# Attention blocks spread over the next projection, with longer rests before their products, in a decoder trunk on one core

## The chip, the cores and the metric

The kernel runs on one core of one Trainium2 chip. The metric is the device time of one execution in microseconds (us), from a median of runs. TensorE (PE in the rows, its weight loads PEld), VectorE (DVE), ScalarE (ACT) and GpSimd (POOL) each work through their own list of instructions; SyncE (SP) issues the DMA transfers.

## The reference, cut to what matters

One decoder layer on 2048 rows of width 1024. The normalised input is projected to 4096 columns, which feed two kinds of head: four HGRN2 heads of 128 (group A) and eight stick-breaking attention heads of 64 (group B). Both outputs are normalised per head, gated, and go through one output projection; a gated embedding is added and a last normalisation ends the layer.

```
# group B: stick-breaking attention, strictly causal
z        = q k^T / 8
log_1m   = where(mask, -softplus(z), 0)
log_rest = cumsum(log_1m, reverse) - log_1m
w        = where(mask, exp(log_sigmoid(z) + log_rest), 0)
o        = w v
# group A: HGRN2, state of 128 x 128 per head
S_t = diag(f_t) S_{t-1} + k_t v_t^T ;  o_t = S_t^T q_t ;  k_t = 1 - f_t
```

## The kernel before, in words

The rows are turned round, so that each query looks forward, and cut into four chunks of 512 (`c` = 3, 2, 1, 0). The 4096 projected columns are cut into eight groups `g` of 512, by turns a pair of B heads and one A head. A **unit** is one group on one chunk: there are 32, four of B, four of A, four of B and so on. Every matmul of f32 numbers is made of three matmuls of f16 parts (high by high, high by low, low by high).

A unit's own work is its **projection** (`proj_A`, `proj_B`): 48 matmuls of 512 columns in `proj_t` and 96 of 256 columns in `proj_n`, written into the PSUM tiles `pj`. What follows on it, the **mix** (`mix_A`, `mix_B`), is written as a Python generator and is emitted piece by piece between the matmuls of the *next* unit's projection. A small planner does this while the program is written. `clock` counts the time of the matmuls emitted so far (columns / 2400 + 0.003 us each, in `mm`). A `yield 4.0` of a generator puts its next piece at least 4.0 of that clock later. `step_tasks` emits the first task whose time has come, and `run` calls it after each step of the projection. A `Task` bears the number of the unit it may run in, and after each projection `drain(u)` emits everything that is still left of that unit's tasks, moving `clock` forward where the next piece isn't due.

The emission order is not the last word: the Tile layer under it orders each engine's instructions once more, by emission and by when it expects their inputs.

`mix_B` works in four blocks of 128 queries. `block(b)` computes two heads' scores `z` against a window of 320 keys (4 matmuls or 8), four sigmoids on ACT (L619, L620), a scan (L624) and a product (L629) on DVE, a cast on ACT (L632), two subtractions on POOL (L634, L636), and a DMA that transposes the weights `wt` into `at` (L638). Then it rests 12.5, and the block's **product** with the values goes into the PSUM tile `op`. Blocks are emitted 4.0 apart. After the fourth product, `finish()` normalises: a square on ACT that reads `op` (L657), a sum on DVE (L659), a power on POOL (L84), a multiplication on POOL (L662) and one on DVE that reads `op` for the last time (L664, into `y_t`). `op` has one buffer (`ps_o`, `bufs=1`), shared by all units of both kinds; `wt` and `at` have two each.

`mix_A` goes through seven levels (12 matmuls `lps` each), with a rest of 2.2 after each, then a transposing DMA of `kp` into `at`, a rest of 6.5, the state matmuls `sp`, and four steps into `op`.

Tasks that prepare weights (`weight_piece`, `prepare_task`) and the input (`prep_x`, in the first four units) run in the same way. After the 32 units a final stage (matmuls `np`) computes the output projection, the embedding and the last normalisation.

Of the kernel before, what the change touches and what calls it, by code (L numbers as in the profile page):

```python
# [8 lines left out]
F32 = mybir.dt.float32  # L9
# [8 lines left out]
P = 128  # L18
# [15 lines left out]
def trunk_kernel(  # L34
# [134 lines left out]
        clock[0] += 0.109  # L169

    class Task:
        def __init__(self, gen, after):
            self.gen, self.ready, self.unit = gen, clock[0] + after, unit[0]

    tasks = []
    unit = [0]

    def spawn(gen, after=0.0):
        tasks.append(Task(gen, after))

    def step_tasks(last):

# [300 lines left out]
    def mix_A(h, c, kq, f_, vh, vl, gs):  # L483
        k_, q_ = kq[:, 0, :], kq[:, 1, :]
        kqf = kq.rearrange("p i t -> p (i t)")
        sc = f32("sc", (P, CB, P))
        pr_ = sc.rearrange("p b t -> p (b t)")
        kp2_ = [f16(f"kp{i}", (P, 2, CH)) for i in range(2)]
        kp = [(t[:, 0, :], t[:, 1, :]) for t in kp2_]
        nc.gpsimd.memset(kp2_[0], 0.0)  # L490
        nc.gpsimd.tensor_tensor(pr_, q_, k_, op=ALU.mult)
        split(kp[1][0], kp[1][1], k_, p2(SKB))
        nc.vector.tensor_tensor(q_, q_, f_, op=ALU.mult)
        v4 = lambda t, B: t.rearrange("p (n h b) -> p n h b", h=2, b=B)
        q3 = lambda t, B: t.rearrange("p (n b) -> p n b", b=B)
        T = {0: f_}
        qc = {}

        def parts(lv):
            B = 1 << lv  # L500
            qc[lv] = f16("qch", (P, CH // 2)), f16("qcl", (P, CH // 2))
            split(q3(qc[lv][0], B), q3(qc[lv][1], B), v4(q_, B)[:, :, 0, :], p2(SQF))
            if lv > 0:
                kh, kl = kp[(lv + 1) % 2]
                split(v4(kh, B)[:, :, 1, :], v4(kl, B)[:, :, 1, :], v4(k_, B)[:, :, 1, :], p2(SKB))

        def update(lv):

            B = 1 << lv
            nb = CH // (2 * B)  # L510
            T2 = T[lv].rearrange("p (n h) -> p n h", h=2)
            act = kqf[:, B : 2 * CH - B].rearrange("p (i m b) -> p i m b", i=2, b=B)[:, :, ::2, :]
            other = T[lv].rearrange("p (n h) -> p h n", h=2).unsqueeze(3).broadcast_to([P, 2, nb, B])
            nc.vector.tensor_tensor(act, act, other, op=ALU.mult)  # L514
            T[lv + 1] = wk.tile([P, nb], F32, name="Tn", tag=f"T{lv}")
            nc.vector.tensor_tensor(T[lv + 1], T2[:, :, 0], T2[:, :, 1], op=ALU.mult)  # L516

        parts(0)
        update(0)
        prh, prl = f16("qh"), f16("ql")  # L520
        split(prh, prl, pr_, p2((SQF + 4)))
        nc.gpsimd.memset(sc, 0.0)
        yield 2.0
        for lv in range(NLEV):
            B = 1 << lv
            kh, kl = kp[(lv + 1) % 2]
            qch, qcl = qc.pop(lv)
            lps = pa("lps", (P, CB, 64))
            for b in range(CB):
                r_ = slice(b * P, (b + 1) * P)  # L530
                s2 = slice(b * 64, (b + 1) * 64)
                mm3(lps[:, b, :], [(kh[:, r_], qch[:, s2]), (kh[:, r_], qcl[:, s2]), (kl[:, r_], qch[:, s2])])
            if lv == 4:
                dps = pa("dps", (P, CB, P))
                mm3(dps, [(ones16, prh), (ones16, prl)])
                nc.vector.copy_predicated(sc, ident.bitcast(I32).unsqueeze(1).broadcast_to([P, CB, P]), dps)
            dst = sc.rearrange("p c (n h b) -> p c n h b", h=2, b=B)[:, :, :, 0, :]
            msk = masks[:, lv, :].bitcast(I16)
            if lv == 0:
                nc.vector.copy_predicated(dst[:, :, :, 0], msk.unsqueeze(1).broadcast_to([P, CB, 64]), lps)  # L540
            elif B == 64:
                nc.vector.copy_predicated(dst[:, :, 0, :], msk.unsqueeze(1).broadcast_to([P, CB, 64]), lps)
            else:
                m4 = q3(msk, B).unsqueeze(1).broadcast_to([P, CB, 64 // B, B])
                nc.vector.copy_predicated(dst, m4, lps.rearrange("p c (n b) -> p c n b", b=B))  # L545
            if lv + 1 < NLEV:
                parts(lv + 1)
                update(lv + 1)
            yield 2.2
        qh, ql = f16("qh"), f16("ql")  # L550
        split(qh, ql, q_, p2(SQF))
        scs = f16("wt", (P, 2, CB, P))
        sch, scl = scs[:, 0], scs[:, 1]
        split(sch, scl, sc, p2(SS - SQF - SKB))
        split(kp[0][0], kp[0][1], k_, p2(SKB))
        ktt = f16("at", (P, 2, CB, P))
        nc.sync.dma_start(ktt.rearrange("p l b d -> p (l b) d"), kp2_[0].rearrange("p l t -> p (l t)"), transpose=True)
        kth, ktl = ktt[:, 0], ktt[:, 1]
        yield 6.5
        sp = ps_t.tile([P, CB, P], F32, name="sp", tag="t")  # L560
        for b in reversed(range(CB)):
            mm3(sp[:, b, :], [(kth[:, b, :], vh[:, b, :]), (kth[:, b, :], vl[:, b, :]), (ktl[:, b, :], vh[:, b, :])])
        op = ps_o.tile([P, CB, P], F32, name="op", tag="o")
        first = c == NC - 1
        if first:
            state[h] = wk.tile([P, P], F32, name="st_")
        st_ = state[h]
        ss = small("ssA", CB)
        for b in reversed(range(CB)):
            r_ = slice(b * P, (b + 1) * P)  # L570
            start_ = first and b == CB - 1
            pairs = [(sch[:, b, :], vh[:, b, :]), (sch[:, b, :], vl[:, b, :]), (scl[:, b, :], vh[:, b, :])]
            if start_:
                nc.vector.tensor_copy(st_, sp[:, b, :])
            else:
                sh = wk.tile([P, P], F16, name="sh", bufs=2)
                sl = wk.tile([P, P], F16, name="sl", bufs=2)
                split(sh, sl, st_, p2(SS - SQF - SKB))
                pairs += [(qh[:, r_], sh), (qh[:, r_], sl), (ql[:, r_], sh)]
                nc.vector.scalar_tensor_tensor(st_, st_, T[NLEV][:, b : b + 1], sp[:, b, :], op0=ALU.mult, op1=ALU.add)  # L580
                yield 1.2
            mm3(op[:, b, :], pairs)
            junk = f16("jk", (P, P))
            nc.scalar.activation(junk, op[:, b, :], AF.Square, accum_out=ss[:, b : b + 1])
        r = rsqrt(ss, CB, 1.0 / P, EPS * p2(2 * (SS + SV)))
        y = f32("y", (P, CB, P))
        for b in range(CB):
            nc.vector.scalar_tensor_tensor(y[:, b, :], op[:, b, :], r[:, b : b + 1], gs[:, b, :], op0=ALU.mult, op1=ALU.mult)
        yield 5.0
        y_out(y, h, c)  # L590
        done(h, c)
# [2 lines left out]
    ZS = p2(-SQ - SK) / 8.0  # L594

    def mix_B(pr, c, qs, kt, gs):
        op = ps_o.tile([P, CB, 2, 64], F32, name="op", tag="o")
        left = [CB]

        def block(b):  # L600
# [35 lines left out]
                nc.gpsimd.tensor_tensor(wt[:, :, WB : 3 * P], sg[:, :, 2 * P :], wt[:, :, 2 * P : WB], op=ALU.subtract)  # L636
            at = f16("at", (P, 2, 5, P))
            nc.sync.dma_start(at.rearrange("p h j t -> p (h j) t"), wt.rearrange("p h s -> p (h s)"), transpose=True)  # L638
            yield 12.5
            for hd in range(2):  # L640
                cols = slice(64 * hd, 64 * hd + 64)
                ah = at[:, hd]
# [9 lines left out]
                spawn(finish())  # L652

        def finish():
            sqt = f32("sc", (P, CB * 2, 64))
            op8 = op.rearrange("p b h d -> p (b h) d")
            nc.scalar.activation(sqt, op8, AF.Square)  # L657
            ss = small("ssB", CB * 2)
            nc.vector.tensor_reduce(ss, sqt, axis=AX, op=ALU.add)  # L659
            r = rsqrt(ss, CB * 2, 1.0 / 64, EPS * p2(2 * (SA + SV)))  # L660
            gr = gs.rearrange("p b (h d) -> p (b h) d", h=2)
            nc.gpsimd.tensor_tensor(gr, gr, r.unsqueeze(2).broadcast_to([P, CB * 2, 64]), op=ALU.mult)  # L662
            y = f32("y", (P, CB, P))
            nc.vector.tensor_tensor(y.rearrange("p b (h d) -> p (b h) d", h=2), op8, gr, op=ALU.mult)  # L664
            yield 7.0
            y_out(y, 4 + pr, c)
            done(4 + pr, c)

        for b in reversed(range(CB)):
            spawn(block(b))  # L670
            yield 4.0


    fin = {}
# [150 lines left out]
    for u, (g, c) in enumerate(order):  # L825
# [2 lines left out]
            w_new(g + 1)  # L828
        for n in ([c - 1, c - 2] if u == 0 else [c - 2]):
            if g == 0 and n >= 0:  # L830
                spawn(prep_x(n), 0.0 if n == c - 1 else 12.0)
        spawn(weight_piece(g + 1, range(KD * i0 // NC, KD * (i0 + 1) // NC)), 3.0)
        kind, i = groups[g]
        unit[0] = u + 1
        run((proj_A if kind == "A" else proj_B)(u, g, i, c), u)
        drain(u)
        if g == 7 and i0 < 3 and c > 0:
            w_new(9 + i0)
            spawn(prepare_task(9 + i0), 0.5)

    for n in range(9, 12):
        if n not in ws:
# [160 lines left out]
```

## Time and profile before

| | us |
|---|---|
| median of 3 runs (lowest, highest) | 1299.4 (1298.64, 1300.02) |
| the profiled execution | 1299.25 |
| its span, first to last instruction | 1297.5 |
| PE busy in the span | 1223.2 |
| DVE, ACT, POOL busy | 870.6, 593.2, 372.5 |

Busy time of PE has modelled ends, since matmuls are pipelined: a 512-column matmul is shown 0.38 us long, while the next starts 0.216 us after it. The stages, by the tiles on PE: start until 50 us, the first B group (with the input's preparation) to 185, A to 280, B to 400, A to 497, B to 610, A to 710, B to 822, the last A group to 960, the final stage to 1290.

### The profile page before, as it was taken

The numbers are of one execution on the slowest core, as the hardware profiler recorded it, in microseconds if no ns is written. First come the engines' busy times: TensorE is split into PE (matmuls) and PEld (weight loads), VectorE is DVE, ScalarE is ACT, GpSimd is POOL, SyncE is SP. The second block draws the span as 40 slices with busy tenths as digits, with TensorE's granted clock in tenths as the row PEclk, the third lists the DMA queues.
The fourth block names the chain that finished last, engine by engine and source line by source line (L and its number), as shares of the span: only waits on it lengthen the run. The fifth ranks groups of instructions, "written<-read, shape, count | busy, mean of one in ns | idle before, by whom it ended". The sixth has DMA issues, their size and how long they took to land.

```text
span 1297.5 us, 25819 instructions
## 1 busy us (share of the span) xinstructions
PE 1223.2 (94%) x9802; PEld 774.3 (60%) x9802; DVE 870.6 (67%) x1736; ACT 593.2 (46%) x1507; POOL 372.5 (29%) x472
## 2 busy tenths in 40 slices
PE   8887989999999999999999999898999999999997
PEld 7655657666666767665776666565544444444443
DVE  5769779986578997567999566799854424324233
ACT  7655534554353454454455444456443323223222
POOL 4247531114442113445111354301022211211112
PEclk9999999999999999999999999999999999999998
DMA  9877640256571025656005557634628226213111
GB/s 262 275 183 182 170 91 14 47 140 134 108 195 28 18 82 131 138 131 139 18 18 135 131 123 171 165 93 141 153 49 186 86 62 154 73 49 110 46 49 52
DMA packets 268964, 147.03 MB, mean 113 GB/s; under 512 B 213280, under 2 KB 237856, under 8 KB 268832
## 3 DMA queue, kind: packets, MB, share of 16 engines
q1 hardware_dynamic: 268688, 145.04, 45.4%
q8 instruction: 79, 1.29, 0.4%
q14 instruction: 53, 0.43, 0.1%
q10 hardware_dynamic: 144, 0.26, 0.1%
HBM read 52.44 MB, written 33.55 MB: 66 GB/s over the span
## 4 chain that ended last, share of the span: by engine, by line
PE 35%; DVE 30%; DMA 13%; issue 7%; ACT 7%; SPq 4%; POOL 3%; ACTq 0%; DVEq 0%; POOLq 0%
PE np L160 27%; PE pj L160 7%; DMA at_t<-wt_t 4%; DVE kq_t L514 4%; DVE kp_t L77 3%; DVE e_t L624 3%; DMA at_t<-kp_t 3%; DVE wl L133 2%; DVE sc_t L545 2%; DVE qcl_t L77 2%; DVE e_t L629 2%; DMA raw_t<-w_in 1%; DVE Tn L516 1%; DVE ys_t L77 1%; POOL wt_t L634 1%
## 5 line engine op out<-in xcount | busy, mean ns | idle before, releaser
L160 PE MATMUL pj<-wh,xh 128*128 128x256 f16 x1024 | 282.6, 276 | 3.1 <-DVE ql_t L77 3.1
L160 PE MATMUL pj<-wh,xl 128*128 128x256 f16 x1024 | 282.4, 276 | 0.0
L160 PE MATMUL pj<-wl,xh 128*128 128x256 f16 x1024 | 282.4, 276 | 0.0
L160 PEld LDWEIGHTS <-xh 128*128 128x128 f16 x2048 | 200.1, 99 | 28.6 <-issue 0.3
L160 PE MATMUL pj<-xh,wh 128*128 128x512 f16 (+1 forms) x560 | 198.3, 365 | 7.5 <-DVE gs_t L389 2.2
L160 PE MATMUL pj<-xl,wh 128*128 128x512 f16 (+1 forms) x560 | 199.0, 365 | 4.2 <-DVE xl L260 3.4
L160 PE MATMUL pj<-xh,wl 128*128 128x512 f16 (+1 forms) x560 | 198.9, 365 | 0.0
L160 PEld LDWEIGHTS <-wh 128*128 128x128 f16 x1120 | 104.4, 99 | 96.3 <-issue 11.9
L160 PEld LDWEIGHTS <-at_t 128*128 128x128 f16 x1688 | 97.3, 98 | 106.6 <-DMA at_t<-wt_t 33.2
L84 POOL TENSOR_TENSOR rs_y<-rs_v,mhalf 128x1 f32<-128x1 f32 (+2 forms) x87 | 82.5, 948 | 269.2 <-DVE rs_v L83 267.1
L160 PE MATMUL np<-wh,fy 128*128 128x512 f16 x512 | 155.7, 379 | 0.0
L160 PEld LDWEIGHTS <-fy 128*128 128x128 f16 x768 | 74.4, 98 | 87.9
L764 DVE TENSOR_TENSOR e_t<-e_t,kq_t 128x512 f32<-128x512 f32 (+2 forms) x33 | 22.3, 675 | 137.4 <-POOL kq_t L763 137.3
L160 PEld LDWEIGHTS <-xl 128*128 128x128 f16 x1024 | 101.3, 99 | 19.9 <-issue 3.8
L624 DVE TENSOR_TENSOR_SCAN e_t<-e_t,reset 128x642 f32<-128x642 f32 x56 | 87.7, 1567 | 24.0 <-ACT e_t L619 23.4
L160 PE MATMUL np<-wh,at_t 128*128 128x512 f16 (+2 forms) x264 | 98.0, 373 | 0.0
L160 PE MATMUL np<-wl,at_t 128*128 128x512 f16 (+2 forms) x264 | 98.0, 373 | 0.0
L160 PE MATMUL np<-wh,wt_t 128*128 128x512 f16 (+2 forms) x264 | 97.9, 373 | 0.0
L160 PE MATMUL np<-wl,fy 128*128 128x512 f16 x256 | 97.0, 379 | 0.0
L76 ACT ACTIVATE qch_t<-kq_t 128x256 f16<-128x256 f32 x112 | 46.8, 418 | 106.2 <-DVE kq_t L514 88.6
L632 ACT CAST wt_t<-e_t 128x640 f16<-128x640 f32 (+1 forms) x64 | 44.9, 701 | 99.5 <-DVE e_t L629 62.0
L634 POOL TENSOR_TENSOR wt_t<-e_t,wt_t 128x512 f16<-128x512 f32 (+1 forms) x64 | 78.1, 1220 | 39.2 <-ACT wt_t L632 39.2
(193 smaller groups left out, 2305.1 us busy)
## 6 DMA issues: line engine op xcount, KB each, us to landing
raw_t<-w_in SPq DMA_DIRECT2D x61, 256.0 KB, 3.6
raw_t<-x_nat SPq DMA_DIRECT2D x56, 256.0 KB, 3.8
out<-y_t SPq DMA_DIRECT2D x31, 256.0 KB, 2.1
kq_t<-x_t SPq DMA_DIRECT2D x12, 512.0 KB, 5.1
bkv<-kn_t SPq DMA_DIRECT2D x64, 64.0 KB, 2.0
bkv<-ql_t SPq DMA_DIRECT2D x64, 64.0 KB, 2.0
bkv<-bkv SPq DMA_DIRECT2D x64, 64.0 KB, 2.3
gs_d<-gs_t SPq DMA_DIRECT2D x16, 256.0 KB, 3.0
```

Of the source, the lines that this page charges most:

```text
L76: nc.scalar.activation(hi, src, AF.Copy, scale=scale)
L77: nc.vector.scalar_tensor_tensor(lo, src, scale, hi, op0=ALU.mult, op1=ALU.subtract)
L84: nc.gpsimd.tensor_tensor(y, v, mhalf[:, 0:n], op=ALU.pow)
L133: nc.vector.scalar_tensor_tensor(self.l[:, k, :], self.r[k], g, self.h[:, k, :], op0=ALU.mult, op1=ALU.subtract)
L160: nc.tensor.matmul(out_, lhsT, rhs, start=start, stop=stop)
L514: nc.vector.tensor_tensor(act, act, other, op=ALU.mult)
L545: nc.vector.copy_predicated(dst, m4, lps.rearrange("p c (n b) -> p c n b", b=B))
L624: nc.vector.tensor_tensor_scan(fl(pr_), fl(f), fl(reset), 0.0, op0=ALU.mult, op1=ALU.max)
L629: nc.vector.tensor_tensor(sg[:, :, :w_], sg[:, :, :w_], pr_[:, :, :w_], op=ALU.mult)
L632: nc.scalar.copy(wt[:, :, :w_], sg[:, :, :w_])
L634: nc.gpsimd.tensor_tensor(wt[:, :, 3 * P : 3 * P + lw], sg[:, :, :lw], wt[:, :, :lw], op=ALU.subtract)
L764: nc.vector.tensor_tensor(h_, h_, p_, op=ALU.add)
```

## The change

Three things are changed in the planner's program; no computation is changed.

1. Rests. `mix_B`: blocks 6.0 apart instead of 4.0, and 16.0 instead of 12.5 between a block's transposing DMA and its product. `mix_A`: 2.4 instead of 2.2 after each of seven levels, 7.0 instead of 6.5 ahead of the state matmuls.
2. The limit. `drain(u - 1)` instead of `drain(u)`: what is left of a mix when its unit ends is emitted within the following unit's projection, and is drained a unit later. Weights and input preparation get `early=1`, and so keep their old limit.
3. `op` of `mix_B` is made at the first product, not at the start of `mix_B`.

```
-        def __init__(self, gen, after):
-            self.gen, self.ready, self.unit = gen, clock[0] + after, unit[0]
+        def __init__(self, gen, after, early):
+            self.gen, self.ready, self.unit = gen, clock[0] + after, unit[0] - early
...
-    def spawn(gen, after=0.0):
-        tasks.append(Task(gen, after))
+    def spawn(gen, after=0.0, early=0):
+        tasks.append(Task(gen, after, early))
... mix_A
-            yield 2.2
+            yield 2.4
...
-        yield 6.5
+        yield 7.0
... mix_B
-        op = ps_o.tile([P, CB, 2, 64], F32, name="op", tag="o")
+        op_ = []
...
-            yield 12.5
+            yield 16.0
+            if not op_:
+                op_.append(ps_o.tile([P, CB, 2, 64], F32, name="op", tag="o"))
+            op = op_[0]
...
         for b in reversed(range(CB)):
             spawn(block(b))
-            yield 4.0
+            yield 6.0
... the loop over units
-                spawn(prep_x(n), 0.0 if n == c - 1 else 12.0)
-        spawn(weight_piece(g + 1, range(KD * i0 // NC, KD * (i0 + 1) // NC)), 3.0)
+                spawn(prep_x(n), 0.0 if n == c - 1 else 12.0, 1)
+        spawn(weight_piece(g + 1, range(KD * i0 // NC, KD * (i0 + 1) // NC)), 3.0, 1)
...
         run((proj_A if kind == "A" else proj_B)(u, g, i, c), u)
-        drain(u)
+        drain(u - 1)
         if g == 7 and i0 < 3 and c > 0:
             w_new(9 + i0)
-            spawn(prepare_task(9 + i0), 0.5)
+            spawn(prepare_task(9 + i0), 0.5, 1)
```

## Rows read from the trace of the kernel before

**Rows 1.** The page: the span, and TensorE's busy time, share, instructions.

```profile
span 1297.5 us, 25819 instructions
PE 1223.2 (94%) x9802; PEld 774.3 (60%) x9802; DVE 870.6 (67%) x1736; ACT 593.2 (46%) x1507; POOL 372.5 (29%) x472
```

**Rows 2.** Busy time by stage: B first, B, A, B, last A, final stage.

```profile
core 0: us, PE busy (x) PEld busy (x) DVE busy (x) ACT busy (x) POOL busy (x), PEclk, DMA share, GB/s
50.00:185.00 135.00, 112.90 (x934) 75.05 (x933) 100.62 (x140) 71.12 (x164) 69.19 (x81) 0.97 0.71 179
280.00:400.00 120.00, 111.85 (x959) 75.87 (x958) 77.83 (x114) 55.76 (x139) 52.75 (x73) 0.97 0.59 135
400.00:497.00 97.00, 95.79 (x997) 69.85 (x996) 91.49 (x225) 48.67 (x136) 14.28 (x13) 1.00 0.21 53
...
710.00:822.00 112.00, 104.53 (x941) 72.61 (x940) 67.94 (x103) 52.23 (x132) 49.28 (x68) 1.00 0.61 135
822.00:960.00 138.00, 130.16 (x1109) 81.31 (x1108) 122.48 (x285) 73.82 (x190) 21.12 (x19) 0.98 0.53 133
960.00:1290.00 330.00, 328.21 (x1555) 150.22 (x1552) 121.13 (x251) 101.23 (x250) 64.58 (x76) 1.00 0.34 84
```

**Rows 3.** Waits of TensorE, whole span: total us, times, longest us.

```profile
PE op L160 <- DMA at_t<-wt_t: 25.3, 21, 3.3
PE op L160 <- DVE y_t L664: 5.6, 3, 2.4
PE lps L160 <- ACT kp_t L76: 4.3, 7, 2.6
...
PE sp L160 <- DMA at_t<-kp_t: 1.9, 4, 0.6
```

**Rows 4.** Timeline near 750 us: one block's scores, its transposing DMA's issue, its product.

```profile
743.74 0.72 PE L160 MATMUL z<-bkv,qs_t 128*128 128x256 f16 x8
...
751.86 1.41 SPq L638 DMA_TRANSPOSE at_t<-wt_t  x1
...
756.26 0.63 PE L160 MATMUL op<-bkv,at_t 128*128 128x64 f16 x16
```

**Rows 5.** Timeline, the block two later: scores, DMA issue, last projections, product.

```profile
752.44 0.71 PE L160 MATMUL z<-bkv,qs_t 128*128 128x320 f16 x4
...
763.14 1.35 SPq L638 DMA_TRANSPOSE at_t<-wt_t  x1
...
765.14 0.38 PE L160 MATMUL pj<-xl,wh 128*128 128x512 f16 x1
766.61 0.26 PE L160 MATMUL op<-bkv,at_t 128*128 128x64 f16 x3 [1.09 <-DMA at_t<-wt_t]
```

**Rows 6.** Timeline from a unit's last product to the next unit's first.

```profile
741.53 0.64 PE L160 MATMUL op<-bkv,at_t 128*128 128x64 f16 x16 [0.71 <-DMA at_t<-wt_t]
...
742.53 0.59 ACT L657 ACTIVATE sc_t<-op 128x512 f32<-128x512 f32 x1
...
748.34 0.68 DVE L664 TENSOR_TENSOR y_t<-op,gs_t 128x512 f32<-128x512 f32 x1
...
751.97 0.63 PE L160 MATMUL op<-bkv,at_t 128*128 128x64 f16 x16
```

**Rows 7.** Timeline, the same pair of events where the chain is slow.

```profile
362.21 0.43 PE L160 MATMUL z<-bkv,qs_t 128*128 128x320 f16 x2
...
366.72 0.63 PE L160 MATMUL op<-bkv,at_t 128*128 128x64 f16 x16
...
381.36 0.67 DVE L664 TENSOR_TENSOR y_t<-op,gs_t 128x512 f32<-128x512 f32 x1
...
382.09 0.84 PE L160 MATMUL op<-bkv,at_t 128*128 128x64 f16 x16 [2.37 <-DVE y_t L664]
```

**Rows 8.** Busy time and granted clock just behind two waits.

```profile
337.95:341.36 3.41, 3.41 (x10) 1.21 (x9) 1.80 (x2) 1.19 (x2) 2.04 (x2) 0.50 0.15 58
382.32:385.74 3.42, 3.42 (x41) 2.75 (x38) 3.42 (x5) 1.10 (x2) 2.19 (x3) 0.50 0.24 58
```

More of the change, by code (lines that the diff above doesn't have):

```diff
@@ L654, in finish @@
         def finish():
+            op = op_[0]
             sqt = f32("sc", (P, CB * 2, 64))
```

## The prediction

> **What bounds the kernel now.** The page comes first: TensorE is busy for 94% of the span [rows 1], so the question is where the other 74 us lie, and whether the change touches them. The view by stage answers the first part [rows 2]. In the final stage PE is busy for 328 of 330 us, and in the A group from 400 to 497 us for 95.8 of 97: there is next to nothing to win there. In the B groups it is busy for 111.9 of 120 and 104.5 of 112 us, and in the first one for 112.9 of 135. So a B group loses some 7 to 8 us of idle PE, the first one 22, and the last A group 8. The same rows show who could take PE's place: in the A group DVE is busy for 91.5 of 97 us, in the B groups for 61 to 65% only.
>
> The view of waits names what ends PE's idle time [rows 3]. The largest entry by far is the product of an attention block that waits for its transposed weights: 25.3 us in 21 waits, the longest 3.3. The product that waits for `y_t`, that is for the single `op` buffer to be read out by the unit before, comes next with 5.6 us in 3 waits.
>
> The timeline shows why. One block's scores start at 743.74 and its product at 756.26 [rows 4]: 12.52 us, which is the planner's rest of 12.5. So the place of a product on PE is set by the rest, as long as PE runs at the planner's pace. Two blocks later the scores start at 752.44, but the transposing DMA is issued only at 763.14, 10.7 us later, and the product waits for it until 766.61, that is 14.2 us after its scores [rows 5]. The rest is thus about as long as the work that it is to cover, and any delay on DVE, ACT, POOL or SP on the way lands on PE. Everything behind the product on PE (the next projection) waits too.
>
> **The change part by part.** The times are summed against the profiled execution's own 1299.25 us, which stands 0.15 us under the median of 1299.4.
>
> *Longer rest and wider spacing in mix_B.* With 16.0 the product stands some 3.5 us later in PE's order, behind projection matmuls that are ready. The longest wait of the 21 is 3.3 us [rows 3], so if the weights arrive no later than now, every one of them is covered. Blocks 6.0 apart also bring fewer chains at once to ACT, DVE and POOL, which should shorten the 10.7 us up to the DMA. Against that, `at` has two buffers: the DMA of block k+2 can't be issued until the product of block k is done. Block k+2 starts 12 after block k, and its DMA comes 8.1 us [rows 4] to 10.7 us [rows 5] into it, at 20 to 23 us of block k; the product of k is done at about 17. That is room of 3 to 6 us, so I take it as free, and SP's queue, in which weight loads and key copies stand behind that DMA, as not held up. I take 2.0 us of the 25.3 as left: -23.3. Bounds: all gone, -25.3; or the waits of the first B group stay, where PE loses 22 us among many late transfers, which I estimate as a third of the 25.3: -17.
>
> *The refill of a wait.* Each wait costs a little more than its idle time: the last projection ahead of one starts at 765.14 and its successor would have started 0.216 later by the planner's formula, at 765.36, but starts at 766.61, so 1.25 us are lost where 1.09 are shown [rows 5]. For 19 waits fewer this is 19 x 0.16 = -3.0.
>
> *The tail into the next unit, and op.* A B unit has 48 matmuls of 512 columns and 96 of 256 (20.9 by the planner's formula) and about 4.1 of scores and products, 25.0 in all. Before, the fourth block started at 12 and its product stood at 24.5; the next unit's first product stood at 25 + 12.5 = 37.5, so `op` had some 13 us to be read out. After, the fourth block starts at about 19 (three spacings of 6.0, each overshooting by about 0.3), its product stands at about 35.9, and the next unit's first one at 25 + 0.6 + 16 + 0.3 = 41.9: `op` has only 6.0 us. What `finish()` needs is in the timeline: from the start of the last product at 741.53 to the end of `y_t` at 748.34 + 0.68 = 749.02 it takes 7.5 us on a good pass [rows 6], and on a bad one 15 us, from the product at 366.72 to the end of `y_t` at 382.03 [rows 7]. So this wait is what is late next. It isn't simply 7.5 - 6.0 at every pass, because PE's order isn't emission alone. At the bad pass the scores of the block start at 362.21; its product starts at 382.09 after a wait of 2.37, so PE had done other work for 17.5 us before it got there, 5 us more than the rest [rows 7]: of an expected lateness of `op`, most is filled with projection, and what is left is where the chip is later than expected. I take 1.0 us at each of the 12 places where one B mix follows another (three in each of four groups), 12.0 instead of 5.6, so +6.4, and +1.5 for nine more refills. Bounds: none at all, -6.1; 2.4 us each, the longest such wait in rows 3, 28.8 - 5.6 + 1.5 = +24.7. I lean to the low side of the middle, since these waits were 1.9 us each and only 3 of them, and the wider spacing relieves the chain.
>
> *The clock.* After the wait at 337 us PE was granted half of its clock (the level of 1.2 GHz) from 337.95 to 341.36, and after the wait of 2.37 at 382.09 from 382.32 to 385.74 [rows 8]. There are four such stretches in B groups behind waits for `at` or `y_t`; each costs half of 3.4, 1.7 us. Two of them gone: -3.4. Bounds: all four, -6.8; none, 0. [...]
>
> *mix_A.* 7 x 0.2 + 0.5 = 1.9 more rest in a mix. Levels and state matmuls stand a little later; the two largest of PE's waits for them are 4.3 + 1.9 us in all [rows 3]. I take -1.5. The A mix is longer than its unit of some 26 us before and after (2.0, seven levels of about 2.5 and 6.5 make 26, and the steps into `op` and `y` come behind), so now its last 8 to 12 us fall among the next unit's projection and beside that unit's own levels, on a DVE that is 94% busy [rows 2]. Bounds -6 and +8, the latter if each of 16 A units makes PE wait half a microsecond.
>
> *Nothing.* The `early` argument keeps weights and input where they were. Making `op` later costs no instruction; made at the start, it would claim the one buffer while the mix before still writes it. The final stage is PE-bound and unchanged.
>
> Sum: -23.3 - 3.0 + 6.4 + 1.5 - 3.4 - 1.5 = -23.3, and 1299.25 - 23.3 = 1276.
>
> **The rivals.**
>
> *Slower: one buffer for op decides.* With 6.0 us between a unit's last product and the next unit's first, and a chain of 7.5 us or more, up to 15 [rows 6, 7], PE could stop at all 12 places, with a half-clock stretch behind about half of them. All other terms together, with the old `y_t` waits gone, give -23.3 - 3.0 - 3.4 - 1.5 - 5.6 = -36.8; over 12 places that is 3.1 us each. A wait of w costs w + 0.16 + 0.85, so from w = 2.1 us on the change loses. At 3 us each it gives 1299.25 - 36.8 + 48 = 1310. For it: the arithmetic of the due times, and that the waits seen were up to 2.4. Against it: the order on PE allows for part of the lateness. The Trainium skill, Perfetto Trace Analysis, section Optimization Strategy, says that the same gap repeating on the engine that should be saturated can mean that there is no free SBUF or PSUM buffer for the next tile; by that rule a longer rest alone would turn one repeated gap into another. The trace bears it out for `op` three times only.
>
> *Half given back.* The products' waits go, but part of it returns: `op` waits of about 1.8 us (+10 against my term), or A levels that come late (+8): 1284 to 1296. For it: DVE at 94% in A groups [rows 2].
>
> *Nothing happens.* If PE's order followed expected readiness and not the rest, the rests would not matter: 1299. Against it: 12.52 us in rows 4, to the hundredth the planner's rest.
>
> *More than forecast.* No `op` waits (-14 against my terms), all four clock stretches gone (-3.4) and a few us less of the 22 that the first B group loses [rows 2]: 1250 to 1267.
>
> **How the numbers follow.** The forecast, 1267 to 1285, has a chance of 0.50, its likeliest value is 1276. More than forecast 0.13, half given back 0.18, nothing happens 0.07, slower 0.12. Within 0.2% means 1296.8 to 1302, about what a measurement of this kernel can tell from no change. So faster 0.81, same 0.07, slower 0.12. The range 1258 to 1299 leaves out about 0.04 below and 0.15 above.
>
> **What would show it.** The waits of `op` for `at_t` should fall from 25.3 us to under 4, in few places. From a block's scores to its product there should be 16.0 to 16.6 us where PE doesn't wait. The waits of `op` for `y_t` should be 5 to 20 us in about a dozen places; above 25 the slower rival holds. PE's idle time in the B groups should fall from 7 or 8 us to about 3, and the A groups should keep their length within 1 us each. The forecast is wrong if `at_t` waits stay above 10 us (then the delay follows the spacing, or the two `at` buffers hold the DMA back), or if the last A group grows by more than 5 us because tails pile up at its end.

## The result, and the profile after

The changed kernel takes 1268.84 us (median of 4 runs, 1265.43 to 1270.64), the kernel before 1299.71 in the same comparison: a ratio of 0.9755, 95% interval 0.9728 to 0.9782, 31 us less. The profiled executions stand at 1265.43 and 1299.25, spans 1263.4 and 1297.5. The profiled execution of the changed kernel is the fastest of its four, 3.4 us under the median, so what is read from the two traces adds up to some 34 us and not to 31.

The page's first lines of the changed kernel, to be set beside [rows 1]:

```profile
span 1263.4 us, 25838 instructions
...
PE 1212.4 (96%) x9802; PEld 775.6 (61%) x9802; DVE 874.3 (69%) x1736; ACT 598.1 (47%) x1507; POOL 361.9 (29%) x472
```

The span is 34.1 us shorter. PE's idle time, span less busy, went from 74.3 to 51.0 us, which is 23.3 of it. The other 10.8 are PE's "busy" time, though it executes the same 9802 matmuls: the modelled tails of matmuls ahead of a wait, and matmuls at half clock, count as busy. The two are estimated further below at 5.8 and 3.4 us. So idle time alone understates what a wait costs.

The view by stage of the changed kernel, for the first B group, a later B group, the A group behind it, and the final stage:

```profile
core 0: us, PE busy (x) PEld busy (x) DVE busy (x) ACT busy (x) POOL busy (x), PEclk, DMA share, GB/s
50.00:172.00 122.00, 107.35 (x878) 73.53 (x877) 101.99 (x134) 69.71 (x162) 68.73 (x79) 0.96 0.77 196
271.30:377.80 106.50, 102.62 (x910) 72.08 (x909) 74.39 (x110) 55.83 (x138) 47.27 (x70) 1.00 0.65 149
377.80:476.80 99.00, 99.00 (x1046) 72.50 (x1045) 94.91 (x229) 51.69 (x140) 16.59 (x17) 1.00 0.23 56
926.00:1256.00 330.00, 328.08 (x1550) 149.99 (x1547) 119.87 (x252) 100.13 (x249) 63.18 (x76) 1.00 0.33 84
```

The first B group has 14.7 us of idle PE where it had 22.1, the B group at 271 us 3.9 where the one at 280 had 8.1 [rows 2]; the A group loses nothing; the final stage is as it was. The groups' lengths, from a B group's first score matmul to the first level matmul of the A group behind it and on to the next B group, tell the same with more detail:

| us | B | A | B | A | B | A | B |
|---|---|---|---|---|---|---|---|
| before | 131.3 | 95.0 | 119.7 | 97.2 | 117.3 | 96.6 | 117.7 |
| after | 118.4 | 99.1 | 106.5 | 99.1 | 108.0 | 99.1 | 106.7 |

B groups are shorter by 46 us in all, the first three A groups longer by 8.5: tails of attention now lie in them. From the last A group's first level matmul to the end of the program it takes 472.8 us against 468.8.

TensorE's waits in the changed kernel, to be set beside [rows 3]:

```profile
PE op L160 <- DVE y_t L668: 14.5, 5, 3.9
...
PE op L160 <- DMA at_t<-wt_t: 3.5, 3, 2.4
PE lps L160 <- ACT kp_t L76: 3.3, 5, 1.7
...
PE sp L160 <- DMA at_t<-kp_t: 0.8, 1, 0.8
```

The products' waits for their transposed weights fell from 25.3 us to 3.5; those for the single `op` buffer rose from 5.6 to 14.5. The timeline shows a usual block and a usual hand-over of `op`: the scores of a block, the last product of the unit before, its square, the block's DMA, the last reading of `op`, the next unit's first product, and the product of the block itself.

```profile
533.04 0.71 PE L160 MATMUL z<-bkv,qs_t 128*128 128x320 f16 x4
...
536.82 0.63 PE L160 MATMUL op<-bkv,at_t 128*128 128x64 f16 x16
...
537.89 0.59 ACT L661 ACTIVATE sc_t<-op 128x512 f32<-128x512 f32 x1
...
540.00 1.33 SPq L638 DMA_TRANSPOSE at_t<-wt_t  x1
...
543.90 0.68 DVE L668 TENSOR_TENSOR y_t<-op,gs_t 128x512 f32<-128x512 f32 x1
...
545.29 0.63 PE L160 MATMUL op<-bkv,at_t 128*128 128x64 f16 x16
...
549.31 0.63 PE L160 MATMUL op<-bkv,at_t 128*128 128x64 f16 x16
```

The DMA of the block at 533.04 is issued 7.0 us after its scores, against 8.1 and 10.7 in [rows 4, 5]; its product stands 16.3 us after them and doesn't wait. `op` is free at 544.58 and wanted at 545.29: 0.7 us to spare, no wait. The five waits for `y_t` lie elsewhere, four of them, one in each group, where the last B mix of the group begins beside the first A unit:

```profile
356.20 0.63 PE L160 MATMUL op<-bkv,at_t 128*128 128x64 f16 x16
...
358.60 0.72 ACT L132 ACTIVATE wh<-raw_t,gm 128x512 f16<-128x512 f32 x1 [2.48 <-DMA raw_t<-w_in]
...
360.06 0.72 ACT L132 ACTIVATE wh<-raw_t,gm 128x512 f16<-128x512 f32 x1 [0.74 <-DMA raw_t<-w_in]
...
361.31 0.59 ACT L661 ACTIVATE sc_t<-op 128x512 f32<-128x512 f32 x1
...
363.97 2.46 POOL L491 TENSOR_TENSOR sc_t<-kq_t 128x512 f32<-128x512 f32 x1 [0.91 <-DVE rs_v L83]
...
366.38 2.22 POOL L84 TENSOR_TENSOR rs_y<-rs_v,mhalf 128x8 f32<-128x8 f32 x1
...
368.72 1.56 POOL L666 TENSOR_TENSOR gs_t<-gs_t,rs_y 128x512 f32<-128x512 f32 x1
...
370.31 0.69 DVE L668 TENSOR_TENSOR y_t<-op,gs_t 128x512 f32<-128x512 f32 x1 [0.93 <-POOL gs_t L666]
...
371.06 0.63 PE L160 MATMUL op<-bkv,at_t 128*128 128x64 f16 x16 [3.88 <-DVE y_t L668]
```

The unit's last product starts at 356.20. The square that could follow at once stands on ACT behind two weight casts, which wait 2.48 and 0.74 us for their loads; the power on POOL stands behind a multiplication of the A mix. So the square starts 4.5 us after the product's end, against 0.4 at the usual hand-over. `op` comes free 14.8 us after the product's start. A group later the same happens to within 0.1 us; in the last group the square is late by 3.1 us, and in the first group the chain loses its time on DVE and POOL. The bad pass of [rows 7] was a hand-over of this kind too.

### The profile page after: what moved, and what is told of

Same layout as the page of the kernel before. It is cut to its first block, busy times and chain, and to the rows that moved or that the text cites. A ratio compares the mean times of both kernels' runs of the same rounds, so it can differ in the third digit from the quotient of the medians.

```text
span 1263.4 us, 25838 instructions
## 1 busy us (share of the span) xinstructions
PE 1212.4 (96%) x9802; PEld 775.6 (61%) x9802; DVE 874.3 (69%) x1736; ACT 598.1 (47%) x1507; POOL 361.9 (29%) x472
## 5 line engine op out<-in xcount | busy, mean ns | idle before, releaser
L84 POOL TENSOR_TENSOR rs_y<-rs_v,mhalf 128x1 f32<-128x1 f32 (+2 forms) x87 | 77.5, 890 | 291.9 <-DVE rs_v L83 236.0
L160 PEld LDWEIGHTS <-at_t 128*128 128x128 f16 x1688 | 100.7, 99 | 91.8 <-issue 15.4
L160 PEld LDWEIGHTS <-wh 128*128 128x128 f16 x1120 | 101.1, 99 | 88.3 <-issue 6.2
L624 DVE TENSOR_TENSOR_SCAN e_t<-e_t,reset 128x642 f32<-128x642 f32 x56 | 87.8, 1567 | 14.4 <-ACT e_t L619 14.1
L160 PEld LDWEIGHTS <-wl 128*128 128x128 f16 x560 | 54.0, 99 | 62.5 <-issue 7.5
```

The lines of the kernel that those rows point to most:

```text
L84: nc.gpsimd.tensor_tensor(y, v, mhalf[:, 0:n], op=ALU.pow)
L160: nc.tensor.matmul(out_, lhsT, rhs, start=start, stop=stop)
L624: nc.vector.tensor_tensor_scan(fl(pr_), fl(f), fl(reset), 0.0, op0=ALU.mult, op1=ALU.max)
```

## The experiments

Each kernel is compared with the kernel before by its ratio; the changed kernel's is 0.9755. The waits are PE's.

| kernel | median us | ratio, 95% interval | op for at_t | op for y_t |
|---|---|---|---|---|
| changed kernel | 1268.8 | 0.9755 (0.9728 to 0.9782) | 3.5 | 14.5 |
| e1 limit alone | 1308.0 | 1.0077 (1.0054 to 1.0099) | 36.5 | 2.2 |
| e2 all but the limit | 1300.6 | 1.0018 (1.0002 to 1.0033) | 17.6 | 4.0 |
| e3 blocks 4.0 apart | 1277.2 | 0.9835 (0.9814 to 0.9856) | 8.5 | 8.5 |
| e4 rest 12.5 | 1267.2 | 0.9749 (0.9715 to 0.9783) | 8.8 | 8.3 |
| e5 mix_A's old rests | 1275.2 | 0.9821 (0.9797 to 0.9844) | 3.3 | 15.0 |
| e6 two buffers for op | 1259.0 | 0.9696 (0.9671 to 0.9721) | 6.0 | none |
| e7 before, two buffers for op | 1300.0 | 1.0001 (0.9980 to 1.0021) | 32.8 | none |
| e8 limit for mix_B alone | 1273.0 | 0.9768 (0.9747 to 0.9790) | 4.8 | 16.2 |
| e9 limit for mix_A alone | 1301.8 | 0.9992 (0.9976 to 1.0007) | 14.4 | 4.8 |
| e10 e6 with rest 12.5 | 1265.8 | 0.9715 (0.9691 to 0.9739) | 21.1 | none |
| e11 e6, longer rests in mix_A | 1261.2 | 0.9677 (0.9657 to 0.9697) | 9.2 | none |
| e12 limit for mix_B and spacing, no more | 1268.0 | 0.9745 (0.9718 to 0.9772) | 8.0 | 8.9 |

The theory at the start was that of the prediction: the longer rest hides the chain from a block's scores to its weights. The rivals were the later limit (tails may fall into the next unit) and the wider spacing of the blocks.

**e1, the limit alone.**

```
-            yield 2.4
+            yield 2.2
...
-        yield 7.0
+        yield 6.5
...
-            yield 16.0
+            yield 12.5
...
-            yield 6.0
+            yield 4.0
```

> The later limit (drain(u - 1), early, op made late) alone, all rests and spacings as before. Theory (the rest is what hides a product's chain): products stand 12.5 us after their scores again, PE's waits of op for at_t stay at 15 to 25 us, the time is 1286 to 1300. Rival (what pays is that a unit's tail is no longer put ahead of the next projection): waits under 8 us, time under 1277.

1308.0: slower than before, with 36.5 us of waits for the weights in 26 places. The limit alone isn't the gain, and the rival falls. Time and waits both lie above what the theory named.

**e2, everything but the limit.**

```
-            self.gen, self.ready, self.unit = gen, clock[0] + after, unit[0] - early
+            self.gen, self.ready, self.unit = gen, clock[0] + after, unit[0] - 0
...
-        drain(u - 1)
+        drain(u)
```

> All rests and spacings of the change, but the old limit: drain(u). Theory (the rest): with blocks 6.0 apart the last two products of each unit are due at 28.6 and 34.9 of 25 and so are put ahead of the next projection; their waits stay, those of the first two go: op for at_t 8 to 16 us, time 1278 to 1290. Rival (the limit is what pays): time 1290 or more.

1300.6, no gain at all: outside what the theory allowed, and on the rival's side. The waits for weights did fall, from 25.3 to 17.6 us, but another entry of the wait view grew:

```profile
PE op L160 <- DMA at_t<-wt_t: 17.6, 15, 2.1
PE lps L160 <- ACT kp_t L76: 12.5, 16, 3.5
```

The level matmuls of A wait 12.5 us where they waited 4.3 before: what the products won, the levels lost. And the timeline shows what draining does to a rest; the scores at 344.29, the DMA at 353.10 and the product at 356.49 are one block's, the other lines are of blocks before it:

```profile
344.29 0.71 PE L160 MATMUL z<-bkv,qs_t 128*128 128x320 f16 x4
...
345.31 1.33 SPq L638 DMA_TRANSPOSE at_t<-wt_t  x1
...
348.33 0.63 PE L160 MATMUL op<-bkv,at_t 128*128 128x64 f16 x16
...
353.10 1.34 SPq L638 DMA_TRANSPOSE at_t<-wt_t  x1
...
354.36 0.63 PE L160 MATMUL op<-bkv,at_t 128*128 128x64 f16 x16
...
356.49 0.64 PE L160 MATMUL op<-bkv,at_t 128*128 128x64 f16 x16 [1.28 <-DMA at_t<-wt_t]
```

The product at 356.49 stands 12.2 us behind its scores, of which 1.28 are a wait: it was placed 10.9 us behind them, not 16. `drain` moves `clock` forward without a matmul, so what it emits ahead of the next projection has no work in front of it to make up the rest. The spacing of 6.0 with the old rests and the old limit was not run, so it isn't shown that the spacing alone gains nothing.

**e3, blocks 4.0 apart, rest 16.0.**

```
             spawn(block(b))
-            yield 6.0
+            yield 4.0
```

> The changed kernel with blocks 4.0 apart again, rest 16.0. Theory (the rest): the chains take up to 14 us as before and 16 covers nearly all of them; op for at_t 3 to 8 us; and op is free for longer (the last product is due at 29.5 instead of 35.9), so its waits for y_t fall from 14.5 to about 6 us; time 1263 to 1273. Rival (the wider spacing shortens the chains, and that is the gain): op for at_t over 12 us, time 1280 or more.

1277.2: 4 us above the theory's range, 3 below the rival's. The waits went the theory's way and came out a little above it (8.5 for the weights, against 36.5 in e1 with the same spacing; 8.5 for `y_t`). At this spacing the longer rests, those of mix_A among them, are worth 31 us (1308.0 to 1277.2).

**e4, rest 12.5, blocks 6.0 apart.**

```
             nc.sync.dma_start(at..., transpose=True)
-            yield 16.0
+            yield 12.5
```

> The changed kernel with a rest of 12.5 again, blocks 6.0 apart. The transposed weights landed 10.0 to 12.6 us after the scores in most blocks of the changed kernel and 15 to 19 us in the last mix of each B group. Theory (the rest): waits of op for at_t come back in the last mix of each group and in the first group, 8 to 14 us in all; time 1274 to 1285. Rival (the spacing is the gain): under 5 us of such waits, time within 4 us of the changed kernel.

1267.2, the same time as the changed kernel, as the rival had it. The theory falls here in its first form: at this spacing the longer rest is worth nothing. The waits agree: those for the weights are 5.3 us higher than in the changed kernel, as the theory had it (8.8, within its 8 to 14), but those for `y_t` are 6.2 us lower. The timeline of a fourth block:

```profile
341.46 0.71 PE L160 MATMUL z<-bkv,qs_t 128*128 128x320 f16 x4
...
349.01 1.90 SPq L638 DMA_TRANSPOSE at_t<-wt_t  x1
...
353.95 0.63 PE L160 MATMUL op<-bkv,at_t 128*128 128x64 f16 x16
```

Its DMA is issued 7.5 us after the scores, and the product stands 12.5 us behind them without a wait. A fourth block of the kernel before had its DMA at 10.7 us and waited [rows 5]. Which engine's shorter queue made the difference was not taken apart.

**e5, mix_A's rests of before.**

```
-            yield 2.4 ... yield 7.0
+            yield 2.2 ... yield 6.5
```

> The changed kernel with mix_A's rests of before (2.2 and 6.5). Theory: they are worth little, PE's waits for lps and sp rise from 6.5 to about 8 us, the time is 0 to 3 us above the changed kernel. Rival (the A groups gained by their longer rests): 5 us or more above it.

1275.2, some 6 us above the changed kernel by the medians and 9 by the ratios: the rival's number. The waits of PE for `lps` and `sp` rose only from 4.1 to 6.7 us, so the waits named don't account for it; e12 below, which has the same old rests, doesn't show it. PE's idle time is 5.9 us more (56.9 against 51.0), spread over many small waits. What the 6 us are is left open.

**e6, two buffers for op.** The PSUM buffer that `sp` had to itself is given to `op`'s pool, and `sp` takes its turns there, with three small tiles used outside the mixes (left out below).

```
-    ps_o = ...(name="ps_o", bufs=1, space=PSUM)
-    ps_t = ...(name="ps_t", bufs=1, space=PSUM)
+    ps_o = ...(name="ps_o", bufs=2, space=PSUM)
...
-        sp = ps_t.tile([P, CB, P], F32, name="sp", tag="t")
+        sp = ps_o.tile([P, CB, P], F32, name="sp", tag="o")
```

> The changed kernel with two PSUM buffers for op; the second is the bank that sp had to itself, so sp and op now take turns in two. Theory (op's one buffer holds the products back): the 14.5 us of waits for y_t go, with 5 refills (0.8) and some 3 us of slow clock; time 1247 to 1256. Rival (the waits move on: to at, whose two buffers are held as long, or to the A groups, where sp and op now share): within 4 us of the changed kernel.

1259.0, about 8 us below the changed kernel by the ratios (0.0059 of 1299.7), less than the theory's 13 to 22 and more than the rival's 4. All 14.5 us of waits for `y_t` are gone; 2.5 us came back as waits for the weights.

**e7, the kernel before with two buffers for op.** The same edit on the kernel before.

> The kernel before with the same two buffers for op and nothing else. Theory: its 5.6 us of waits for y_t go, with 3 refills and two stretches of half clock (3.4): 1290 to 1294, and the waits for at_t stay at about 25 us. Rival (op's buffer also set the late products, so more goes): under 1286.

1300.0, no change; both expectations missed. The waits for `y_t` are gone, and those for the weights rose from 25.3 to 32.8 us. In two of the last mixes of a group it shows how: the first product no longer waits for `op`, and the second, which didn't wait before, now comes ahead of its weights:

```profile
385.85 0.71 PE L159 MATMUL op<-bkv,at_t 128*128 128x64 f16 x16 [3.45 <-DMA at_t<-wt_t]
...
600.60 0.64 PE L159 MATMUL op<-bkv,at_t 128*128 128x64 f16 x16 [2.74 <-DMA at_t<-wt_t]
```

**e8 and e9, the limit for one kind of mix.**

```
e8: -        spawn(mix_A(h, c, kq, f_, vh, vl, gs))
    +        spawn(mix_A(h, c, kq, f_, vh, vl, gs), 0.0, 1)
e9: -        spawn(mix_B(pr, c, qs, kt, gs))
    +        spawn(mix_B(pr, c, qs, kt, gs), 0.0, 1)
```

> The changed kernel, but mix_A keeps the old limit: only the tails of attention may fall into the unit after. With all tails cut the gain was gone (1300.6) and PE waited 12.5 us for lps and 17.6 us of op for at_t. Theory (both kinds of tail matter, each by its own waits): the waits for lps come back to about 10 us, those of op for at_t stay near 4; time 1276 to 1288. Rival (all of the gain is attention's tail): within 4 us of the changed kernel.

> The complement: mix_B keeps the old limit, only mix_A's tails may fall into the unit after. Theory: the waits of op for at_t are at 14 to 18 us, those for lps under 5; time 1280 to 1290. Rival (A's tails are the gain): within 4 us of the changed kernel.

e8 takes 1273.0, 0.0013 above the changed kernel in the ratio and inside its interval; e9 takes 1301.8, as before. So the limit matters for attention's tails alone, and without it nothing is gained. The theory's guess about `lps` was wrong the other way round: they wait 3.0 us in e8, where mix_A is drained at its unit's end, and 12.1 us in e9, where mix_B is (e8 first, then e9):

```profile
PE lps L160 <- ACT kp_t L76: 3.0, 4, 1.4
...
PE lps L160 <- ACT kp_t L76: 12.1, 20, 3.5
```

In e9 as in e2 the A levels wait longer when attention keeps the old limit. How the one leads to the other was not tested.

**e10 and e11, on top of two buffers.** e10 is e6 with the rest of 12.5; e11 is e6 with 2.6 and 7.5 in mix_A.

> Two PSUM buffers for op as in the run before, and the rest of 12.5 again with blocks 6.0 apart. With one buffer the rest of 16.0 was worth nothing (1267 against 1269), since waits for at_t fell by 5 us and those for y_t rose by 6. Theory (op's one buffer took the rest's gain back): with two buffers the rest is worth its at_t waits, so this kernel is 4 to 9 us above the one with two buffers and 16.0, 1263 to 1268. Rival (beyond 6.0 apart the rest is of no use at all): within 3 us of it.

> Two buffers for op, and mix_A's rests lengthened once more, to 2.6 and 7.5. The first lengthening was worth 6 us. Theory (A's levels wait on a DVE that is nearly full, and more room helps until its tail fills the next unit): 0 to 4 us below the one with two buffers, 1254 to 1259. Rival (A's tail now meets the next unit's own levels): 2 us or more above it.

e10 takes 1265.8, a median inside the theory's 1263 to 1268, but the kernel before took 1301.5 beside it and 1299.7 beside e6. By the ratios it is 0.0019 above e6, in intervals that overlap: 2.5 us, which is the rival's side. The waits for the weights are 21.1 us against 6.0, so with `op` free the short rest does leave products waiting; most of that doesn't show in the time (all of PE's idle gaps together are 42.4 us against 35.2). e11's median is 2.2 us above e6's and its ratio, 0.9677, 2.5 us below, also in overlapping intervals. The two are the fastest kernels of the study; which of them is faster isn't settled, and so neither is e11's theory or rival.

**e12, two edits on attention and no more.** The kernel before with the limit for mix_B and blocks 6.0 apart; rest 12.5, mix_A's rests and limit as before (`op` is made late, as in every run but e7).

```
-        drain(u)
+        drain(u - 1)
...
-        spawn(mix_A(h, c, kq, f_, vh, vl, gs))
+        spawn(mix_A(h, c, kq, f_, vh, vl, gs), 0.0, 1)
...
             spawn(block(b))
-            yield 4.0
+            yield 6.0
```

> The kernel before with two edits on attention alone: its tails may fall into the unit after, and its blocks stand 6.0 apart. Its rest is 12.5 again, and mix_A keeps its rests and its limit of before. From the runs so far the rest is worth 0, mix_A's limit 2 us and its rests 6 us. Theory (these add up): 1274 to 1282, with waits of op for at_t near 9 us and for y_t near 8. Rival (these two edits are the whole gain): within 3 us of the changed kernel.

1268.0, ratio 0.9745: the changed kernel's time. The rival holds: these two edits are enough for the whole gain, and e1, with the limit and without the spacing, has none of it. The waits are those of e4, as expected (8.0 and 8.9).

## Why the prediction was right, and where it was not

The time lies at the lower edge of the forecast's own band, 1267 to 1285, with the predicted sign; by profiled executions the change is -33.8 us where the sum gave -23.3. That it lies inside the band is in part luck: the change carried a wider spacing and a later limit along with the rest that the forecast was built on, and those two brought the gain.

*Longer rest and wider spacing in mix_B (-23.3).* The size was right: -21.8. The cause was not. The prediction put it to the 16.0 and took the wider spacing as a help. e4 and e12 reach the same time with 12.5, since most blocks 6.0 apart get their weights in time for it (8.8 and 8.0 us of waits are left). e3 shows that the rest does the same work on the waits when the blocks stay 4.0 apart, 36.5 to 8.5 us. The two are substitutes, each enough for most of the waits. That the two `at` buffers would not hold the DMA back held for most blocks, not for all: in the first unit of each later group the third block's DMA is issued 0.45 us after the first block's product starts (295.07 and 294.62), though PE doesn't wait there. In the second and third units of the later groups a product stands 16.3 to 16.7 us behind its scores, the first of each unit 18.4 us, about what the prediction asked for.

*The tail into the next unit, and op (+6.4 and +1.5).* This is the step that failed. The tail was booked as a cost of the change, by way of `op`. The runs show it to be a condition of the gain: with the rests and the spacing of the change, but without the later limit for attention (e2, e9), there is none. In e2 a drained product was placed 10.9 us behind its scores, and the 7.7 us that the products' waits lost came back as 8.2 us of waits of A's levels; why the levels wait is open. The prediction had the means to see the first half: the fourth product was due at 35.9 of a unit of 25. On `op` itself the size was near, +8.9 instead of +6.4, but not as 1.0 us in 12 places: six usual hand-overs have 0.7 us to spare each, and PE's order gave them 8.5 us between products instead of the 6.0 worked out; four places beside A's first unit take 13.6 of the 14.5 us, where the engines of the chain have other work ahead of it.

*Slower: one buffer for op decides.* The mechanism was real and too small: 14.5 us of waits, below the 25 at which it would have decided, and e6 gains 8 us by its removal. The Trainium skill, Perfetto Trace Analysis, section Optimization Strategy, says that a repeated gap can mean a missing buffer; here part of the gap did move to a buffer, as that rival had it (5.6 to 14.5 us), but mainly at four places, not at every unit. e7 shows that in the kernel before the same buffer was not what held PE.

*The refill of a wait (-3.0, and +1.5 for those of op).* Mis-sized: PE's idle gaps above 60 ns, without the one at the program's start, went from 69 to 33 in the two traces, and 36 x 0.16 gives an estimate of -5.8 us against -1.5.

*The clock (-3.4).* Right in size, by luck: between 50 and 960 us there were seven stretches at half clock before and five after, two times 1.7 us. But they are not the same ones: new ones stand behind waits for `y_t`, as at 577.29, and the one behind the wait at 371.06 did not come.

```profile
577.29:580.70 3.41, 3.41 (x30) 2.69 (x29) 3.38 (x6) 0.78 (x3) 0.81 (x4) 0.50 0.37 76
```

*mix_A (-1.5).* The two waits named fell from 6.2 to 4.1 us, about as said. The A groups were to keep their length within 1 us and grew by 2 to 4: two of the four products of the last attention mix now stand behind the group's first level matmul. The last A group, with the final stage, grew by 4.0 us, short of the 5 that would have been a sign of a wrong forecast.

*What the sum left out.* Of PE's 23.3 us less idle time, -21.8 and +8.9 are the two waits above; so -10.4 came from PE's other waits, all but a few under 2 us and some of them longer than before; the sum held 1.5 of it for mix_A. The scores' wait for `e_t`, 3.1 us in the first group and not in the sum, is gone; several others fell by 1 or 2 us each. With the refills this is most of the 10 us by which the gain exceeded the forecast.

## What to carry to other kernels

When work is emitted with rests between other work, look first at what happens at the limit where the rest must end: pieces pushed out there lose their rest, and longer rests then move more pieces over the limit. A rest and a spacing can do the same job, so price them one by one with the other held, in both settings: here the spacing, with the limit moved, gave the whole gain, the longer rests, mix_A's among them, gave two thirds of it, and together they gave no more. A wait that is removed shows whether a second one stood just behind it: two buffers for `op` were worth nothing before the change and 8 us after it.

## What the runs showed of the hardware that was not expected

The power on POOL (L84) took 0.55 us for one element per partition and 1.64 us for eight, both as medians in the kernel before, so its 0.95 us on the page is a mean of different shapes. In the chain shown above it took 2.22 us for eight, and the multiplication ahead of it (L491) 2.46 us where its median in the changed kernel is 1.64; what slows them there was not tested. And the longest waits don't always cost clock. Behind the wait of 3.88 us at 371.06 the granted clock stayed full (1.00 for the two stretches from 271.30 to 476.80, the level of 2.4 GHz). Behind its twin a group later, of 3.85 us, came the half-clock stretch from 577.29 shown above:

```profile
576.54 0.63 PE L160 MATMUL op<-bkv,at_t 128*128 128x64 f16 x16 [3.85 <-DVE y_t L668]
```

Before the change such a stretch stood behind a wait of only 2.37 us at 382.09 [rows 7, 8]. So in these traces the length of a wait doesn't tell by itself whether the clock falls.
